# Eight chains a step for the latents' scan, and a new order of the work in its gaps

## The chip, the cores and the metric

The kernel runs on one core of a Trainium2 chip. The metric is the device time of one execution in microseconds. The engines are named as the profile names them: PE (TensorE, matrix products; PEld are its weight loads), DVE (VectorE), ACT (ScalarE), POOL (GpSimd) and SP (SyncE, which here only issues transfers). ACT and POOL issue transfers too; those of POOL go through a software queue, those of SP and ACT through hardware queues.

## The reference

One layer of a block with two branches over 1024 latent tokens that follow 256 context tokens, width 1024, all in float32. One input projection feeds both branches; branch A is RWKV-7 time mixing with 16 heads of 64, in both directions, branch B is retention. Sigmoid gates merge them, and an output projection follows.

```python
def step(S, inp):                       # branch A, one token
    w_t, k_t, v_t, kk_t, b_t = inp[:5]
    sa = jnp.einsum('bhvk,bhk->bhv', S, kk_t)
    S = (S * w_t[:, :, None, :] - sa[..., None] * b_t[:, :, None, :]
         + v_t[..., None] * k_t[:, :, None, :])
    o = jnp.einsum('bhvk,bhk->bhv', S, inp[5]) if with_out else None
    return S, o
...
o = head_norm((outs[0] + outs[1]).reshape(B, L, A_WIDTH), ln_w, ln_b, A_HEADS, A_GN_EPS)
...
merged = jax.nn.sigmoid(ma) * ya + jax.nn.sigmoid(mb) * yr
x = x + gate[:, None, :] * (merged @ w_out[l])
```

The latents' scans start from the final state of the context's scan in the same direction, so 32 scans (16 heads, two directions) of 1280 tokens are run.

## The kernel before

**Stages.** By the time of the span: projections and the preparation of branch A (0 to 820 us); the scans over the context, filled with the matmuls of retention's values, gv (820 to 1172); the scans over the latents, filled with the matmuls of the gates, gm (1172 to 1772); retention and the output of branch A (1772 to 2180); the output projections (to 2480). The change lies in the second and third stage, above all in the third.

**Scans in chunks.** A scan is cut into chunks of 64 tokens. Two heads share the 128 partitions; such a pair in one direction is a chain here, 8 pairs times 2 directions. A chunk's products between keys (A, in `chunk_mats`) are masked by DVE into ka (64 rows) and aa (128 rows); keys bk are then scaled by POOL and turned by PE against the identity (bt, in `chunk_turn`), with ACT moving them to SBUF. For each set of four chunks of eight pairs and directions the inverses of triangular matrices are needed: `inv_keys` makes the products B, `inv_vec` runs 31 pairs of operations (tmp, TL) and twelve 32x32 turns (E, TD, TN) on DVE, and `inv_join` makes the full inverses T from their quarters by two rounds of small products I. T is put together by ACT's copies.

**A step.** `chain_step` takes some chains one chunk further: X = keys times state sv, negated by ACT (xs); U = T times xs, copied by ACT (uv), with O, the queries' product with the state; S = the turned keys times uv, added by DVE to the decayed state sp (made by POOL) into the next sv, with O's second part. After each of the three products `gap()` flushes stores of finished gates and fills in as many gate matmuls as the remaining ones divided by the remaining gaps, so that PE has work while ACT and DVE make the next operand. Here a step has four chains (two pairs, two directions), 64 steps are run, and there are 192 gaps with some six gm each. The lambdas handed to `chain_step` put the next chunks' A, bt and the inverses' work into the gaps: `inv_gap(t)` counts 24 gaps for each inverse, calls `inv_keys` five times and `inv_join` twice in them and doles out `inv_vec` over about 24.

**What sets the order.** The kernel is written in a language where a scheduler orders instructions by dependencies and priorities, but `late` adds an order: an operation marked so comes on its engine behind the last PE instruction, or behind the last one that `lead` named for "v" (DVE) or "a" (ACT). So the lead operations (sv, xs, uv) stand ahead of what was written after them with `late(.., "v")`, such as the inverses' tmp and TL, whereas the masks were not leads. Pools limit the buffers: pA has four PSUM buffers (for A, bt, B, I), gates have three gp buffers on the way to memory.

**Outputs.** Outputs of four chains and two chunks leave PSUM together; `put` copies (first half of the groups) or adds (second half, when the two directions meet) into oT, a buffer of all 1024 tokens of two pairs, which is stored once per two pairs, by SP and at the end by POOL.

Of the kernel before, what the change touches and what calls it, by code (L numbers as in the profile page):

```python
# [49 lines left out]
MF = 3.0  # L50
# [78 lines left out]
class Kern:  # L129
# [588 lines left out]
    def v_proj(self, dst, hi, lo):  # L718

        nc = self.nc  # L720
        for t in range(0, 10, 2):
# [14 lines left out]
            nc.scalar.dma_start(dst[t * P:(t + 2) * P, :].rearrange("(i q) c -> q i c", q=P), st)  # L736
# [62 lines left out]
    def subs(self, n):  # L799

        if n < 2:
            return [(p, d, 0) for p in range(4 * n, 4 * n + 4) for d in range(2)]
        pp, half = divmod(n - 2, 2)
        return [(p, d, NCU + 8 * half + 4 * q) for q in range(2) for p in (2 * pp, 2 * pp + 1) for d in range(2)]
# [83 lines left out]
    def inv_vec(self, job):  # L888
# [22 lines left out]
        for i in range(0, 32, 8):  # L911
# [6 lines left out]
            self.late(nc.scalar.copy(t[b:b + 32, :, 0:32], tdq[b:b + 32]), "a")  # L918
            yield TV
# [5 lines left out]
    def inv_join(self, job):  # L925

        nc, ts, tn = self.nc, job["t2"], job["TN"]
        pis = [self.pA.tile([P, 16, 32], F32, tag="A", name=self.nm("I")) for _ in range(2)]
        at = lambda q, b: 64 - b if q else b
        for l in range(16):  # L930
            for q, t in enumerate(ts):
                for b in (0, 64):
                    o = at(q, b) + 32
                    self.mm(pis[q][o:o + 32, l, :], t[b:b + 32, l, 32:64], tn[b:b + 32, 16 * q + l, :], start=True, stop=True)
        for q, t in enumerate(ts):
            for b in (0, 64):
                o = at(q, b) + 32
                self.late(nc.scalar.mul(t[b + 32:b + 64, :, 0:32], pis[q][o:o + 32], -1.0), "a")
        yield
        pis = [self.pA.tile([P, 16, 32], F32, tag="A", name=self.nm("I")) for _ in range(2)]  # L940
        for l in range(16):
            for q, t in enumerate(ts):
                for b in (0, 64):
                    o = at(q, b)
                    self.mm(pis[q][o:o + 32, l, :], t[b + 32:b + 64, l, 0:32], t[b + 32:b + 64, l, 32:64], start=True, stop=True)
        for q, t in enumerate(ts):
            for b in (0, 64):
                o = at(q, b)
                self.late(nc.scalar.copy(t[b:b + 32, :, 32:64], pis[q][o:o + 32]), "a")
                nc.gpsimd.memset(t[b + 32:b + 64, :, 0:32], 0.0)  # L950
        yield

    def inv_gap(self, t):
# [26 lines left out]
        if g == 16:  # L980
# [3 lines left out]
    def chunk_loads(self, p, u0, d=None, extra=False):  # L984
# [4 lines left out]
        odd = p % 2 if d is None else d  # L989
        ka = (self.wp if extra else rw).tile([P, 3, 4, C], F32, tag=f"ka{odd}", name=self.nm("ka"), bufs=2 - extra)  # L990
# [6 lines left out]
        two = lambda t: t.rearrange("q (d u) c -> q d u c", d=2)  # L997
        nc.sync.dma_start(two(bk), self.bkD[p].rearrange("d q u c -> q d u c")[:, :, u0:u0 + 2, :])
        o = C * (u0 - NCU)
        kr = lambda rows, a: self.krD[p, :, rows, a, o:o + 2 * C].rearrange("d q j -> q d j")  # L1000
        pair = lambda t: t.rearrange("q (d u) c -> q d (u c)", d=2)
        for h, ch, va in self.HEADS:
            nc.sync.dma_start(pair(ka[ch, 2 * h]), kr(ch, 0))
        nc.sync.dma_start(pair(ka[:, 1]), kr(slice(0, P), 1))
        scale = self.pc[:, p, :, u0:u0 + 2].rearrange("q d (u o) -> q d u o", o=1)
        return bk, ka, scale, False

    def chunk_mats(self, loads):
# [5 lines left out]
        if ctx:  # L1014
# [6 lines left out]
            nc.gpsimd.tensor_tensor(bk, bk, scale.broadcast_to([P, 4, 2 * C]), op=ALU.mult)  # L1021
        else:
# [3 lines left out]
            for i in range(4):  # L1026
                for h, ch, va in self.HEADS:
                    self.mm(pas[h][:, i], bk[ch, i, :], ka[ch, h:h + 2, i, :], start=True, stop=True)
            for h, ch, va in self.HEADS:
# [3 lines left out]
                nc.vector.tensor_tensor(aa[:, h], pa[:, :, 1 - h], m, op=ALU.mult)  # L1033
            b4 = bk.rearrange("q (d u) c -> q d u c", d=2)
            nc.gpsimd.tensor_tensor(b4, b4, scale.broadcast_to([P, 2, 2, 2 * C]), op=ALU.mult)
# [3 lines left out]
    def chunk_turn(self, mats):  # L1039
# [6 lines left out]
        for h in range(2):  # L1046
            nc.scalar.mul(bt[:, :, C * h:C * h + C], pt[:, :, C * h:C * h + C], self.mask[:, 3 * C + h:3 * C + h + 1])

    def chain_step(self, chains, sv, uv, pcs, extra, new=None, out=None):
# [4 lines left out]
        nc, rw = self.nc, self.rw  # L1054
        px = self.pC.tile([P, 4, C], F32, tag="C", name=self.nm("X"))
# [3 lines left out]
        xs = rw.tile([P, 4, C], F32, tag="xs", name=self.nm("xs"), bufs=1)  # L1059
# [538 lines left out]
```

## Time and profile before

| | us |
|---|---|
| median of 3 runs (lowest, highest) | 2477.68 (2475.95, 2483.03) |
| the profiled execution, own time | 2481.7 |
| its span | 2479.9 |
| mean granted clock of TensorE | 0.989 |
| PE, PEld busy over the span | 2384.1, 1925.7 |
| DVE, ACT, POOL busy | 1597.4, 1162.4, 576.3 |

Busy times are shares of one span and overlap. A row of the profile gives the engine, the line, the operation, the result and the operands by their names in the program, and then busy time, mean duration, and the idle time before it with what ended it. A float32 matmul of one kind shows two records. A line L557 is the helper `mm`, so that groups are told apart by the names of the tiles.

### The profile page before, as it was taken

How to read it: one execution, taken by the hardware profiler on the slowest of the kernel's cores; microseconds unless marked ns; L12 is line 12 of the kernel's file. 1: busy time of each engine (PE TensorE's matmuls, PEld its weight loads, DVE VectorE, ACT ScalarE, POOL GpSimd, SP SyncE). 2: the span in 40 equal slices, each digit the busy share in tenths (PEclk: the TensorE clock that was granted, in tenths of full speed). 3: DMA queues.
4: the chain of work that ended last, by engine and by line, in shares of the span. 5: the costliest groups of instructions: out<-in, count | busy, mean ns of one | idle time of the engine just before them, and what ended most of it. 6: DMA issues, size and time to landing. Idle time of an engine off the chain costs nothing. (4 is left out here: it accounts for less than half of the span.)

```text
span 2479.9 us, 53486 instructions
## 1 busy us (share of the span) xinstructions
PE 2384.1 (96%) x21200; PEld 1925.7 (78%) x21200; DVE 1597.4 (64%) x2834; ACT 1162.4 (47%) x2547; POOL 576.3 (23%) x720
## 2 busy tenths in 40 slices
PE   7999999999999999998999999999898998999998
PEld 4888888888888899987777777777666765688786
DVE  5486787777676244353988878783278657754644
ACT  6444344434443434445665556644356435543422
POOL 2221111112122011221222222223276335400000
PEclk9999999999999999998999999999899999999999
DMA  6154454455346625344555565553465654585552
GB/s 252 50 158 116 140 165 124 135 157 140 124 136 182 194 79 147 106 133 129 171 164 169 155 189 168 155 159 117 124 194 169 214 169 151 180 287 170 186 171 85
DMA packets 337708, 385.07 MB, mean 155 GB/s; under 512 B 87466, under 2 KB 240818, under 8 KB 334386
## 3 DMA queue, kind: packets, MB, share of 16 engines
q1 hardware_dynamic: 304370, 298.80, 39.2%
q0 software_dynamic: 12992, 55.58, 8.5%
q10 hardware_dynamic: 20096, 27.27, 3.1%
q8 instruction: 167, 2.74, 0.5%
q14 instruction: 83, 0.68, 0.1%
HBM read 264.63 MB, written 116.92 MB: 154 GB/s over the span
## 5 line engine op out<-in xcount | busy, mean ns | idle before, releaser
L330 PE MATMUL gm<-uh,wh 128*128 128x512 f32 x896 | 351.9, 394 | 5.3 <-ACT xp L402 3.3
L331 PE MATMUL gm<-ul,wh 128*128 128x512 f32 x896 | 352.1, 393 | 0.8 <-DVE ul L299 0.8
L332 PE MATMUL gm<-uh,wl 128*128 128x512 f32 x896 | 351.6, 392 | 0.0
L1065 POOL TENSOR_TENSOR sp<-sv,pc 64x256 f32<-64x256 f32 x152 | 105.0, 691 | 418.1 <-DVE sv L1089 197.9
L330 PEld LDWEIGHTS gm<-uh,wh 128*128 128x128 f32 x896 | 168.5, 188 | 39.7 <-ACT xp L402 3.7
L331 PEld LDWEIGHTS gm<-ul,wh 128*128 128x128 f32 x896 | 168.8, 188 | 38.1 <-issue 1.7
L332 PEld LDWEIGHTS gm<-uh,wl 128*128 128x128 f32 x896 | 168.6, 188 | 34.5
L660 DVE TENSOR_TENSOR wlo<-wraw,whi 128x256 fp32r<-128x256 f32 x168 | 79.4, 487 | 144.5 <-ACT whi L659 141.6
L557 PE MATMUL gm<-uh,wlo 128*128 128x512 f32 x416 | 171.2, 411 | 0.7 <-DVE wlo L660 0.7
L557 PE MATMUL gm<-uh,whi 128*128 128x512 f32 x416 | 171.4, 412 | 0.0
L557 PE MATMUL gm<-ul,whi 128*128 128x512 f32 x416 | 170.8, 411 | 0.0
L557 PE MATMUL gv<-wlo,uh 128*128 128x256 f32 x512 | 147.8, 289 | 1.5 <-issue 1.5
L557 PE MATMUL gv<-whi,ul 128*128 128x256 f32 x512 | 148.0, 289 | 0.0
L211 DVE TENSOR_TENSOR lo<-raw,hi 128x512 fp32r<-128x512 f32 x128 | 93.0, 731 | 85.4 <-ACT hi L210 85.2
L557 PE MATMUL gv<-whi,uh 128*128 128x256 f32 x512 | 147.8, 289 | 0.0
L210 ACT CAST hi<-raw 128x512 fp32r<-128x512 f32 x128 | 78.9, 622 | 140.4 <-PE yr L1277 76.2
L902 DVE TENSOR_TENSOR tmp<-E,TL 128x31 f32<-128x31 f32 (+15 forms) x310 | 131.0, 423 | 8.9
L904 DVE TENSOR_TENSOR TL<-TL,tmp 128x31 f32<-128x31 f32 (+15 forms) x310 | 128.2, 414 | 8.2
L1477 PE MATMUL ro<-s,rs 128*128 128x512 f32 x256 | 123.8, 596 | 4.8 <-DVE s L1431 4.4
L1079 ACT COPY uv<-U 64x256 f32<-64x256 f32 x160 | 58.8, 367 | 146.5 <-PE U L557 87.3
L1089 DVE TENSOR_TENSOR sv<-S,sp 64x256 f32<-64x256 f32 x144 | 60.7, 422 | 98.3 <-PE S L557 65.4
L210 ACT CAST wh<-wr 128x1024 fp32r<-128x1024 f32 x56 | 58.8, 1051 | 132.6 <-PE gm L331 104.6
(297 smaller groups left out, 6206.9 us busy)
## 6 DMA issues: line engine op xcount, KB each, us to landing
wr<-in_w_in SPq DMA_DIRECT2D x56, 512.0 KB
wraw<-in_w_in SPq DMA_DIRECT2D x84, 256.0 KB
bk<-bkD SPq DMA_DIRECT2D x80, 256.0 KB
krD<-kr POOLq DMA_DIRECT2D x16, 1024.0 KB, 4.6
raw<-in_wr SPq DMA_DIRECT2D x64, 256.0 KB
vtD<-vt POOLq DMA_DIRECT2D x64, 160.0 KB, 4.2
bkD<-bk POOLq DMA_DIRECT2D x32, 320.0 KB, 6.7
bkD<-bk POOLq DMA_DIRECT2D x16, 640.0 KB, 6.5
```

What stands on the lines that cost most here:

```text
L210: nc.scalar.copy(hi, src)
L211: (eng or nc.vector).tensor_tensor(lo, src, hi.bitcast(F32), op=ALU.subtract)
L330: nc.tensor.matmul(acc[:, :n], hi[:, k, :], self.hi(k, t0, n), start=(k == 0), stop=False)
L331: nc.tensor.matmul(acc[:, :n], hi[:, k, :], self.lo(k, t0, n), start=False, stop=False)
L332: nc.tensor.matmul(acc[:, :n], lo[:, k, :], self.hi(k, t0, n), start=False, stop=(k == KT - 1))
L557: return self.pin(self.nc.tensor.matmul(*a, **k))
L660: self.late(nc.vector.tensor_tensor(lo[:, j % size, k:k + 2], r, h.bitcast(F32), op=ALU.subtract), "v")
L902: self.late(nc.vector.tensor_tensor(t3, et[:, j + 1:, j:j + 1].broadcast_to([P, n, m]), tl[:, j:j + 1, 0:m].broadcast_to([P, n, m]), op=AL ...
L904: self.late(nc.vector.tensor_tensor(tl[:, j + 1:, 0:m], tl[:, j + 1:, 0:m], t3, op=ALU.subtract), "v")
L1065: nc.gpsimd.tensor_tensor(sp[ch], sv[ch, h], pcs[ch].broadcast_to([64, 4, C]), op=ALU.mult)
L1089: self.lead("v", nc.vector.tensor_tensor(new[h], ps[ch], sp[ch], op=ALU.add))
L1477: nc.tensor.matmul(po, qx[d][:, k, cols], st[:, k, :], start=(d == 1 and k == 0), stop=False)
```

## The change

1. A step has eight chains, four pairs with two directions, and one chunk: 32 steps, 96 gaps with twice the matmuls. `subs`, `lat_loads`, `lat_values`, `chunk_loads`, `chain_step` and `rwkv_lat` follow; loads take pieces of one chunk where they took two.
2. A is computed in two halves of 64 columns; the masks for aa become leads of DVE, the copies of bt leads of ACT. In a step's first gap stand A of the next chunks' first half and all turns of the next step's keys (`turns`), in the second the other half's A (`products`), in the third the outputs (`outputs`).
3. `inv_gap` counts 12 gaps for an inverse and doles out `inv_vec` over ten of them. `inv_join` makes its first round in gap 11 and its second in the next step's `turns`, each cut in the middle by `fill(0.6)`, three gm. Half of T's copies go from ACT to POOL.
4. Stores of gates and of values are issued by POOL in place of ACT.
5. oT becomes og, of two chunks and four pairs, stored every second step by POOL and, for the second half, loaded back by SP ahead of the addition.
6. MF, the filling between the pieces at the head of the latents, goes from 3.0 to 5.0.

On PE, a step in the midst of the latents before. X, A, U, O, B and S are the products named above, gm a gate matmul; the last number is how many like rows follow each other:

```order
L557 MATMUL X_14789<-sv_14316,ka_14141 64x64 x4
L557 MATMUL X_14789<-sv_14316,ka_14296 64x64 x4
L557 MATMUL A_14804<-ka_14614,bk_14613 128x128
L557 MATMUL A_14805<-ka_14614,bk_14613 128x128
...
L557 MATMUL gm_14786<-uh_97,wlo_14158 128x512
...
L557 MATMUL U_14839<-xs_14798,T_1314_11686 64x64 x2
L557 MATMUL O_14627<-ka_14141,sv_14316 64x64 x2
...
L557 MATMUL S_14912<-uv_14317,bt_14352 64x64 x4
```

and after:

```order
L557 MATMUL X_13977<-sv_13658,ka_13513 64x64 x8
L557 MATMUL X_13977<-sv_13658,ka_13519 64x64 x8
L557 MATMUL A_14000<-ka_13819,bk_13818 64x128
L557 MATMUL A_14001<-ka_13819,bk_13818 64x128
...
L1038 MATMUL bt_14024<-ident,bk_13512 128x128 x4
L1038 MATMUL bt_14031<-ident,bk_13518 128x128 x4
L557 MATMUL gm_13896<-ul_110,whi_13441 128x512
...
L557 MATMUL U_14062<-xs_13994,T_1246_11301 64x64 x2
L557 MATMUL O_13976<-ka_13513,sv_13658 64x64 x2
...
L557 MATMUL A_14098<-ka_13825,bk_13824 64x128
```

Blocks of X, U and O have twice the matmuls, an A has sixteen rows of 64 columns in place of eight of 128, both turns follow the first A, and the second A follows U and O; between A or the turns and the next block stand twelve gm where there were six or seven.

On DVE, between two updates of the state (sv) before, in a gap with the inverses' work:

```order
L1089 TENSOR_TENSOR sv_11924<-S_12394,sp_12293 64x4x64 x2
...
L660 TENSOR_TENSOR wlo_12430<-wraw_12433,whi_12429 128x256
L902 TENSOR_TENSOR tmp_12714<-E_12552,TL_12553 128x31
L904 TENSOR_TENSOR TL_12553<-TL_12553,tmp_12714 128x31
...
L702 SCALAR_TENSOR_TENSOR gp_12614<-gp_12614,gm_12427 128x512
L1032 TENSOR_TENSOR ka_12474<-A_12596,mask 64x256
L1033 TENSOR_TENSOR aa_12595<-A_12596,mask 128x256
```

and after, from one sv to the next masks:

```order
L1083 TENSOR_TENSOR sv_14316<-S_14652,sp_14347 64x512 x2
L902 TENSOR_TENSOR tmp_14689<-E_14479,TL_14480 128x192
...
L1224 TENSOR_TENSOR og_14323<-O_14322,og_14323 128x4x64 x2
...
L904 TENSOR_TENSOR TL_14480<-TL_14480,tmp_14698 128x21x11
L1026 TENSOR_TENSOR ka_14568<-A_14746,mask 64x256
L1027 TENSOR_TENSOR aa_14745<-A_14746,mask 128x256
...
L902 TENSOR_TENSOR tmp_14784<-E_14479,TL_14480 128x240
```

The inverses' operations of a gap stand behind the masks of that gap, and there are more of them in it.

On POOL, after (before, its queue in this stage held sp, bk and the memsets and, at its end, the last stores of oT):

```order
L1060 TENSOR_TENSOR sp_13685<-sv_13348,pc 64x512 x2
L1232 DMA oD<-og_12955 64x4x128 x4
L711 DMA grD<-gp_13650 128x512
L1028 TENSOR_TENSOR bk_13512<-bk_13512,pc 128x512
...
L918 COPY T_1313_11730<-TD_13882 32x16x32 x2
L918 COPY T_1314_11731<-TD_13882 32x16x32 x2
```

The stores of gates and outputs and half of T's copies now stand in one queue with sp and bk.

The diff, cut to its core:

```diff
-MF = 3.0
+MF = 5.0
...
-                self.begin(gates, 3 * 16 * NPAIR // 2, 0.0)
+                self.begin(gates, 3 * 16 * NPAIR // 4, 0.0)
...
-            self.late(self.nc.scalar.dma_start(dst, st), "a")
+            self.nc.gpsimd.dma_start(dst, st)
...
-            nc.scalar.dma_start(dst[t * P:(t + 2) * P, :].rearrange("(i q) c -> q i c", q=P), st)
+            nc.gpsimd.dma_start(dst[t * P:(t + 2) * P, :].rearrange("(i q) c -> q i c", q=P), st)
...
-            self.late(nc.scalar.copy(t[b:b + 32, :, 0:32], tdq[b:b + 32]), "a")
-            yield TV
+            nc.gpsimd.tensor_copy(t[b:b + 32, :, 0:32], tdq[b:b + 32])
+            yield 2 * TV
...
+        for first in (True, False):
+            pis = [self.pA.tile([P, 16, 32], F32, tag="A", name=self.nm("I")) for _ in range(2)]
+            for l in range(16):
+                if l == 8:
+                    self.fill(0.6)
+                for q, t in enumerate(ts):
+                    for b in (0, 64):
+                        o = at(q, b) + 32 * first
+                        lhs, rhs = (t[b:b + 32, l, 32:64], tn[b:b + 32, 16 * q + l, :]) if first else \
+                            (t[b + 32:b + 64, l, 0:32], t[b + 32:b + 64, l, 32:64])
+                        self.mm(pis[q][o:o + 32, l, :], lhs, rhs, start=True, stop=True)
             for q, t in enumerate(ts):
                 for b in (0, 64):
+                    o = at(q, b) + 32 * first
+                    if first:
+                        self.late(nc.scalar.mul(t[b + 32:b + 64, :, 0:32], pis[q][o:o + 32], -1.0), "a")
+                    else:
+                        self.late(nc.scalar.copy(t[b:b + 32, :, 32:64], pis[q][o:o + 32]), "a")
+                        nc.gpsimd.memset(t[b + 32:b + 64, :, 0:32], 0.0)
+            yield
...
-        per, g = divmod(t, 24)
+        per, g = divmod(t, 12)
         last = 1 + NPAIR
         n = 4 + per
-        if g == 1 and n <= last:
+        if g == 0 and n <= last:
             self.jobs[n] = {}
             self.keys = self.inv_keys(n, self.jobs[n], self.wp)
-        if g in (1, 4, 7, 10, 13) and n <= last:
+        if g in (0, 1, 4, 7, 10) and n <= last:
             next(self.keys)
-        if g in (19, 22) and 3 + per <= last:
-            if g == 19:
-                self.join = self.inv_join(self.jobs[3 + per])
+        if g == 11 and 3 + per <= last:
+            self.join = self.inv_join(self.jobs[3 + per])
             next(self.join)
-        if t == 0 or g == 17:
-            n = 3 + per + (g == 17)
+        if g == 0:
+            n = 3 + per
             self.vec = self.inv_vec(self.jobs[n]) if n <= last else iter(())
-            self.vec_us, self.vec_gaps, self.owed = 12 * TV + sum(map(self.sub_us, range(31))), 24 if t else 17, 0.0
+            self.vec_us, self.vec_gaps, self.owed = 16 * TV + sum(map(self.sub_us, range(31))), 10, 0.0
         self.owed += self.vec_us / self.vec_gaps
         while self.owed > 0.0:
             us = next(self.vec, None)
             if us is None:
                 break
             self.owed -= us
-        if g == 16:
+        if g == 9:
...
-        two = lambda t: t.rearrange("q (d u) c -> q d u c", d=2)
-        nc.sync.dma_start(two(bk), self.bkD[p].rearrange("d q u c -> q d u c")[:, :, u0:u0 + 2, :])
+        nc.sync.dma_start(bk, self.bkD[p:p + 2, :, :, u0, :].rearrange("a d q c -> q (a d) c"))
         o = C * (u0 - NCU)
-        kr = lambda rows, a: self.krD[p, :, rows, a, o:o + 2 * C].rearrange("d q j -> q d j")
-        pair = lambda t: t.rearrange("q (d u) c -> q d (u c)", d=2)
+        kr = lambda rows, a: self.krD[p:p + 2, :, rows, a, o:o + C].rearrange("a d q j -> q (a d) j")
         for h, ch, va in self.HEADS:
-            nc.sync.dma_start(pair(ka[ch, 2 * h]), kr(ch, 0))
-        nc.sync.dma_start(pair(ka[:, 1]), kr(slice(0, P), 1))
-        scale = self.pc[:, p, :, u0:u0 + 2].rearrange("q d (u o) -> q d u o", o=1)
+            nc.sync.dma_start(ka[ch, 2 * h], kr(ch, 0))
+        nc.sync.dma_start(ka[:, 1], kr(slice(0, P), 1))
+        scale = self.pc[:, p:p + 2, :, u0:u0 + 1].rearrange("q a d o -> q (a d) o")
...
-                for h, ch, va in self.HEADS:
-                    self.mm(pas[h][:, i], bk[ch, i, :], ka[ch, h:h + 2, i, :], start=True, stop=True)
+                for c in (slice(0, C), slice(C, 2 * C)):
+                    for h, ch, va in self.HEADS:
+                        self.mm(pas[h][c, i], bk[ch, i, c], ka[ch, h:h + 2, i, :], start=True, stop=True)
...
-                nc.vector.tensor_tensor(aa[:, h], pa[:, :, 1 - h], m, op=ALU.mult)
-            b4 = bk.rearrange("q (d u) c -> q d u c", d=2)
-            nc.gpsimd.tensor_tensor(b4, b4, scale.broadcast_to([P, 2, 2, 2 * C]), op=ALU.mult)
+                self.lead("v", nc.vector.tensor_tensor(aa[:, h], pa[:, :, 1 - h], m, op=ALU.mult))
...
-            nc.scalar.mul(bt[:, :, C * h:C * h + C], pt[:, :, C * h:C * h + C], self.mask[:, 3 * C + h:3 * C + h + 1])
+            self.lead("a", nc.scalar.mul(bt[:, :, C * h:C * h + C], pt[:, :, C * h:C * h + C], self.mask[:, 3 * C + h:3 * C + h + 1]))
...
+            def turns():
+                if s != 8:
+                    self.send(outs)
+                if n and n % 4 == 0:
+                    next(self.join, None)
+                if n < last:
                     nxt.append(self.chunk_mats(ld.pop(0)))
+                for m in mats:
+                    self.chunk_turn(m)
+                self.inv_gap(3 * n)
+
+            def products():
+                if n < last:
+                    nxt.append(self.chunk_mats(ld.pop(0)))
+                    if n + 1 < last:
+                        ld.extend(self.lat_loads(n + 2, a) for a in range(2))
+                self.inv_gap(3 * n + 1)
+
+            def outputs():
+                self.put(po, og, s)
+                if s % 2:
+                    outs.append((r, s, og))
+                if s == 7:
+                    self.send(outs)
+                self.inv_gap(3 * n + 2)
+            if s % 2 == 0:
+                og = self.wp.tile([P, 2, 4, 2, C], F32, tag="og", name=self.nm("og"), bufs=2)
+                if s >= 8:
+                    self.move(r, s + 1, og, nc.sync, True)
+            self.chain_step(chains, sv, uv, pcs, (turns, products, outputs), dst, po)
...
+    def put(self, po, og, s):
+        src = po.rearrange("p (a d) c -> p a d c", d=2)
+        for dst, x in ((og[:, 0, :, s % 2], src[:, :, 0]), (og[:, 1, :, 1 - s % 2], src[:, :, 1][:, :, ::-1])):
+            if s < 8:
+                self.nc.scalar.copy(dst, x)
             else:
+                self.nc.vector.tensor_tensor(dst, x, dst, op=ALU.add)
+    def move(self, r, s, og, eng, load):
+        for d, t0 in ((0, C * (s - 1)), (1, LAT - C * (s + 1))):
+            for h, ch, va in self.HEADS:
+                mem = self.oD[4 * r:4 * r + 4, ch, t0:t0 + 2 * C].rearrange("p q t -> q p t")
+                sb = og[va, d].rearrange("q p u c -> q p (u c)")
+                eng.dma_start(*((sb, mem) if load else (mem, sb)))
+    def send(self, outs):
+        for r, s, og in outs:
+            self.move(r, s, og, self.nc.gpsimd, False)
+        outs.clear()
```

More of the change, by code (lines that the diff above doesn't have):

```diff
@@ L802, in subs @@
             return [(p, d, 0) for p in range(4 * n, 4 * n + 4) for d in range(2)]
-        pp, half = divmod(n - 2, 2)
-        return [(p, d, NCU + 8 * half + 4 * q) for q in range(2) for p in (2 * pp, 2 * pp + 1) for d in range(2)]
+        r, q = divmod(n - 2, 4)
+        return [(p, d, NCU + 4 * q) for p in range(4 * r, 4 * r + 4) for d in range(2)]
     def inverse(self, n):
@@ L931, in inv_join @@
             for q, t in enumerate(ts):
                 for b in (0, 64):
[L933 to L950, printed above, removed]
@@ L1072, in chain_step @@
             if out is not None:
-                po, first, last = out
                 for h, ch, va in self.HEADS:
-                    self.mm(po(va, ci), sv[ch, h, ci, :], rho[ch], start=(first and ci == 0), stop=False, skip_group_check=True)
+                    self.mm(out[va, ci], sv[ch, h, ci, :], rho[ch], start=(ci == 0), stop=False, skip_group_check=True)
         with self.tc.high_priority(offset=URGENT):
@@ L1092, in chain_step @@
                 for h, ch, va in self.HEADS:
-                    self.mm(po(va, ci), uv[:, h, ci, :], aa[:, h, :], start=False, stop=(last and ci == 3), skip_group_check=True)
+                    self.mm(out[va, ci], uv[:, h, ci, :], aa[:, h, :], start=False, stop=(ci == m - 1), skip_group_check=True)
         extra[2]()
@@ L1134, in chain_ctx @@
             else:
-                end = rw.tile([P, 4, C], F32, tag="xs", name=self.nm("send"), bufs=1)
+                end = rw.tile([P, 8, C], F32, tag="xs", name=self.nm("send"), bufs=1)[:, :4]
                 dst = [end[ch] for h, ch, va in self.HEADS]
@@ L1226, in put @@
-    def put(self, po, oT, g):
-        nc = self.nc
-        f = oT[:, :, P * g:P * g + P]
-        r = oT[:, :, LAT - P * g - P:LAT - P * g][:, :, ::-1]
-        for d, o in enumerate((f, r)):
-            src = po.rearrange("p (a d) u c -> p a d (u c)", d=2)[:, :, d]
-            if g < 4:
-                nc.scalar.copy(o, src)
-            else:
-                nc.vector.tensor_tensor(o, src, o, op=ALU.add)
+        last, og, outs = 2 * 16 - 1, None, []
+        for n in range(last + 1):
+            r, s = divmod(n, 16)
+            t2 = self.t2[2 + 4 * r + s // 4]
+            chains = [(ka[:, :, i], ka[:, 1, i], aa[:, :, i], bt[:, i], t2[a][:, 4 * i + s % 4, :])
+                      for a, (ka, aa, bt, bk) in enumerate(mats) for i in range(4)]
+            sv, uv = vals
+            if n < last:
+                vals = self.lat_values(n + 1)
+            dst = [vals[0][ch, h] for h, ch, va in self.HEADS] if s < 15 else None
+            pcs = self.pc[:, 4 * r:4 * r + 4, :, NCU + s:NCU + s + 1].rearrange("q p d o -> q (p d) o")
+            po = self.pO.tile([P, 8, C], F32, tag="O", name=self.nm("O"))
+            nxt = []
+            def turns():
[4 more added lines that the diff above has]
+                if n < last:
+                    nxt.append(self.chunk_mats(ld.pop(0)))
+                for m in mats:
+                    self.chunk_turn(m)
+                self.inv_gap(3 * n)
+            def products():
+                if n < last:
+                    nxt.append(self.chunk_mats(ld.pop(0)))
[14 more added lines that the diff above has]
+            self.chain_step(chains, sv, uv, pcs, (turns, products, outputs), dst, po)
+            mats = nxt
```

97 lines of the change are left out of this document (27 added, 70 removed).

## The prediction

> **What bounds the kernel now.** I read the page first (span, engine totals), then busy time by stage, then the waits of TensorE in the stage that the change rewrites, and last the timeline of one of its steps.
>
> ```profile
> span 2479.9 us, 53486 instructions
> ```
>
> ```profile
> 1172.00:1772.00 600.00, 588.53 (x10050) 459.50 (x10051) 447.99 (x1045) 337.06 (x895) 163.72 (x209) 1.00 0.54 156
> ```
>
> The columns after the length are the busy times of PE, PEld, DVE, ACT and POOL, then the granted clock, the DMA share and GB/s. The second row is the stage of the latents' chains: PE is busy for 588.5 of 600 us at clock 1.00, DVE for 448, ACT for 337, POOL for 164. So here only PE's own time counts, and what would make PE wait. The waits of PE in these 600 us are small:
>
> ```profile
> PE B L557 <- DMA bi<-bkD: 5.1, 5, 2.0
> PE S L557 <- issue: 3.5, 4, 1.0
> PE X L557 <- DVE sv L1089: 1.4, 2, 1.1
> ```
>
> Hence the gain must come from PE's order itself. One step of four chains, by the start of each group:
>
> ```profile
> 1401.53 0.69 PE L557 MATMUL X<-sv,ka 128*64 128x64 f32 x16
> 1402.15 1.16 PE L557 MATMUL A<-ka,bk 64*128 64x128 f32 x16
> 1403.24 0.50 PE L557 MATMUL gm<-uh,wlo 128*128 128x512 f32 x1
> 1403.58 0.40 PE L557 MATMUL gm<-uh,whi 128*128 128x512 f32 x1
> 1403.81 0.39 PE L557 MATMUL gm<-ul,whi 128*128 128x512 f32 x1
> ...
> 1404.73 0.39 PE L557 MATMUL gm<-uh,wlo 128*128 128x512 f32 x1
> 1405.05 0.27 PE L557 MATMUL U<-xs,T 64*64 64x64 f32 x2
> 1405.06 0.27 PE L557 MATMUL O<-ka,sv 64*64 64x64 f32 x2
> 1405.15 0.23 PE L557 MATMUL U<-xs,T 64*64 64x64 f32 x2
> ...
> 1405.52 0.23 PE L557 MATMUL O<-ka,sv 64*64 64x64 f32 x2
> 1405.67 0.50 PE L557 MATMUL gm<-uh,whi 128*128 128x512 f32 x1
> ...
> 1406.94 0.40 PE L557 MATMUL gm<-uh,wlo 128*128 128x512 f32 x1
> 1407.27 0.69 PE L557 MATMUL S<-uv,bt 128*64 128x64 f32 x16
> 1407.78 0.64 PE L557 MATMUL O<-aa,uv 128*64 128x64 f32 x16
> 1408.35 0.66 PE L1045 MATMUL bt<-ident,bk 128*128 128x128 f32 x4
> ...
> 1410.32 0.39 PE L557 MATMUL X<-sv,ka 128*64 128x64 f32 x6
> ```
>
> Busy times overlap, so I use distances between starts. Within a stretch of gate matmuls (gm) they are 0.23 apart (1403.58 to 1403.81). The first one takes 0.34 (1403.24 to 1403.58), and from the last one to the next small product pass 0.32 (to U) or 0.33 (to S). A stretch thus costs 0.11 + 0.09 = 0.20 us beside its matmuls. The step is 8.79 us (1401.53 to 1410.32), and there are 64.
>
> **Fewer, longer gaps: what PE saves.** Eight chains a step leave the number of X, U, O, S, A and gm matmuls as it is; they stand in half as many blocks. Gaps go from 192 to 96; each of the 14 halves of the seven joins is cut by three gm, which adds 14 stretches. 192 - 110 = 82 fewer, times 0.20: -16.4 us. The blocks have an opening of their own. X takes 0.62 for 16 records (1401.53 to 1402.15) and S, behind the same kind of gap, 0.51; I take 0.12 of X as opening, 32 X blocks fewer: -4. U with O: eight quadruples, 0.10 for the first and about 0.06 for each later one ((1405.52 - 1405.15) / 6), closed by 0.15 to the gm. Two such blocks become one, which saves 0.04 + 0.15 a pair; in 31 steps the second A, in tiles of the same 64x64 kind, stands right behind it, and I take another 0.07 there: -0.26 x 32 = -8.3. S with O: 0.51 + 0.57, of which I take 0.15 as the turn from one kind of block to another, 31 fewer: -4.7. The gm inside the joins cause 14 more switches: +2. Sum -31.4.
>
> **The A product in halves.** 16 records of 64x128 tiles take 1.09 us (1402.15 to 1403.24), two tiles side by side; after, 32 records in 64x64 tiles. That U and O of both heads start 0.01 apart and a whole quadruple takes 0.06 says that four 64x64 tiles run together; then the same columns stream for the same time. Bounds: 0, and 1.09 more for each of 62 products (one pair of tiles at a time). I take 0, since the U/O rows are the same form.
>
> **Inverses in 10 of 12 gaps, masks and transposed keys first.** Ahead, the work of one inverse on DVE was spread over about 24 gaps; now ten gaps of twice the length carry it, that is 3.33 of every 4 steps.
>
> ```profile
> L902 DVE TENSOR_TENSOR tmp<-E,TL 128x31 f32<-128x31 f32 (+15 forms) x217 | 97.3, 449 | 6.1
> L904 DVE TENSOR_TENSOR TL<-TL,tmp 128x31 f32<-128x31 f32 (+15 forms) x217 | 94.2, 434 | 5.6
> L1032 DVE TENSOR_TENSOR ka<-A,mask 64x256 f32<-64x256 f32 x124 | 51.7, 417 | 17.2 <-PE A L557 15.6
> ...
> L896 DVE STREAM_TRANSPOSE E<-D 128x256 f32<-128x256 f32 x28 | 15.5, 607 | 13.6 <-ACT D L883 12.9 <-ACT T L918 0.5
> ```
>
> An inverse has 31 pairs of L902 and L904 (0.883 us, 27.4) and twelve turns like L896 (0.607, 7.3): 34.7 us, 10.4 a loaded step. All else on DVE is 448 - 7 x 34.7 = 205 us, 6.4 for each of 32 steps. So DVE needs 16.8 us in a step of about (600 - 31) / 32 = 17.8: 94%. It does not bind on the mean, but the masks (two products, four operations each, 0.42 apiece), the states sv and the outputs' additions come in clumps; masks ahead of the inverses' work now end before the next gap's work starts, and sv, queued on DVE behind tmp and TL, is what comes late: the next step's X waits for it, and with X the whole of PE. Bounds 0 and +30 (the second rival); I take 0.35 in each of 23 loaded steps, +8.
>
> **Joins and PSUM.** Seven times the second half of a join, two products and two turns share the four pA buffers within two gaps; the turns wait for ACT to empty the join's two.
>
> ```profile
> L918 ACT COPY T<-TD 32x512 f32<-32x512 f32 x28 | 17.3, 618 | 0.3
> ...
> L949 ACT COPY T<-I 32x512 f32<-32x512 f32 x28 | 16.2, 578 | 2.5 <-PE I L557 2.1
> ```
>
> Four L949 copies are 2.3 us; the product between hides about 1.1 of that and the masks' own wait part of the rest. Bounds 0 and 7 x 2.3 = 16; I take 0.7 each, +5. Half of the T copies (28, 0.62 us each on ACT) go to GpSimd: ACT loses 17 us that no one waits for.
>
> **Stores and outputs.** ACT loses 51 gate stores and SP most of 16 stores of outputs; POOL gets the former, 64 shorter stores of outputs, and the copies. POOL is busy for 164 of 600 us, so it has room, and three gp buffers give the stores a delay of some 11 us (24 gm of 0.23 a buffer, two buffers ahead). SP gets 32 loads of the outputs' first half, each asked for long before the addition; the store that the first of them needs was sent a step earlier. The keys, values and outputs now travel in pieces of half the size; the DMA share of 0.54 leaves room. Late landings I put at +3 (bounds 0 and 10). Of the old waits shown above, 10 us, I let all go: the keys are loaded elsewhere and a longer gap covers the states; if they stay, that is the upper end.
>
> **The start of retention.** SP's five loads of rs take 36 us there, and the waits of SP's queue name the gate stores; TensorE waits at the end of that chain.
>
> ```profile
> 1743.44 36.08 SPq L1388 DMA_DIRECT2D rs<-kD  x5
> ```
>
> ```profile
> SPq L1388 <- DMA maD<-gp: 18.4, 2, 9.8
> ```
>
> ```profile
> PE st L1416 <- ACT kx L1401: 12.3, 4, 8.8
> ```
>
> With the gate stores on GpSimd's queue the loads need not wait for ACT's. Bounds 0 and -8.8; I take -5. MF at 5.0 and the vst stores move fills and issues within the two heads, where the same number of gm is run later or earlier: 0, between -4 and +4.
>
> **Sum.** -31.4 for PE's order, +8 +5 +3 -10 for waits, -5 for retention: -30.4. The profiled execution took 2481.7 us (span 2479.9), 4.0 above the median of 2477.68 of the three runs. 2481.7 - 30.4 = 2451.3 profiled, 2447 against the median.
>
> **Rivals.** (1) *No new waits.* The masks are the only thing that TensorE needed early and they now come first; then +8 +5 fall away: 2434. For it speaks the 6% that DVE has left, against it the clumps.
> (2) *DVE becomes the bound.* In these rows GpSimd and DVE hold each other up:
>
> ```profile
> 1402.96 0.41 DVE L902 TENSOR_TENSOR tmp<-E,TL 128x240 f32<-128x240 f32 x1
> 1403.40 0.41 DVE L904 TENSOR_TENSOR TL<-TL,tmp 128x240 f32<-128x240 f32 x1
> 1403.85 1.14 DVE L902 TENSOR_TENSOR tmp<-E,TL 128x247 f32<-128x247 f32 x1
> ```
>
> ```profile
> 1403.48 1.24 POOL L1035 TENSOR_TENSOR bk<-bk,pc 128x512 f32<-128x512 f32 x1 [1.67 <-issue]
> ```
>
> The tmp that starts inside a scaling of bk takes 0.73 longer. A step has four such GpSimd operations (two bk, two sp). If every one stops an inverse's operation for 0.73, that is 2.9 a step; 0.6 of it is in the means already ((0.449 - 0.41 + 0.434 - 0.41) x 31 / 3.33). DVE then needs 16.8 + 2.3 = 19.1 of 17.8 us, +1.3 in 23 loaded steps: +30 in place of the +8 that I took, 2469, at the edge of what can be told from no change. It decides once the collisions cost over 1 us a step. Against it: the T copies come when DVE turns TN, and the masks read PSUM.
> [...]
> (3) *Slower: A's halves do not run four abreast.* With one pair of tiles at a time a product takes 2.18 in place of 1.09 us: +68 for 62, 2515. It decides from 30.4 / 62 = 0.49 us more a product. The U/O rows speak against it; they have 64 columns a record and A has 128.
> (4) *The change does nothing for retention:* the rs loads wait for something else; 2452, inside the range.
>
> **Chances.** Forecast with (4) 0.52, rival 1 0.23, rival 2 0.13, rival 3 0.07, others (a late store or load that blocks a buffer over and over) 0.05. A change of 0.3%, 7.4 us, is about what a measurement tells here: faster is below 2470.2, slower above 2485.1. Faster 0.81: the forecast, rival 1 and half of rival 2; same 0.09, the other half and some of the others; slower 0.10, rival 3 and the rest of the others. The range goes from just below rival 1, 2431, to a little beyond rival 2, 2474.
>
> **What would show it.** Right: some 36 gm a step in three long stretches; A 32 records in 1.1 us; X 32 records in about 1.1; the stage some 25 to 32 us shorter; PE's waits in it 15 to 20 us, led by sv and by the A or bt that waits for T copies; the 8.8 us wait of st shrunk. Wrong: A records with starts 2.2 us apart in all; waits on sv or masks beyond 30 us; DVE without idle time in loaded steps; or waits on GpSimd's stores.

## The result and the profile after

The changed kernel takes 2467.66 us, the median of 5 runs (2460.66 to 2468.66); the kernel before took 2483.01 us in the 5 runs beside them (2475.95 to 2483.11). The ratio is 0.9929 with a 95% interval from 0.9911 to 0.9946: faster by 0.7%, about 17 us (the two medians are 15.4 us apart). The forecast was 2447 us and a gain of 30.7: the sign and the range held, the size was nearly twice too large. Part of the distance in microseconds is the base: the three runs shown ahead of the change had a median of 2477.68, later medians of the same kernel were 2481.5 to 2483.9. So the profiled execution of before, 2481.7 us, did not stand above the median, and the 4.0 us that the forecast took off for it were wrong. The rest is in the trace.

Span, engine totals and clock of the changed kernel, as on the page of before:

```profile
span 2465.6 us, 55584 instructions
PE 2356.7 (96%) x22224; PEld 1927.3 (78%) x22224; DVE 1570.7 (64%) x2774; ACT 1120.5 (45%) x2411; POOL 682.8 (28%) x852
PEclk9999999999999899989999999999999999999999
```

PE is busy 27 us less than before. More instructions stand on it, the halves of A. Busy time by stage, the first row of before, the others of after (length; PE, PEld, DVE, ACT, POOL; granted clock, DMA share, GB/s):

```profile
820.00:1172.00 352.00, 335.16 (x4374) 313.24 (x4375) 141.62 (x360) 158.01 (x430) 48.89 (x68) 0.98 0.45 129
```

```profile
820.00:1172.00 352.00, 336.27 (x4355) 314.63 (x4355) 140.03 (x359) 143.41 (x395) 87.16 (x121) 0.95 0.44 126
1172.00:1772.00 600.00, 567.37 (x11121) 467.76 (x11119) 430.55 (x994) 317.98 (x806) 236.42 (x293) 0.99 0.69 178
```

Fixed stretches mix the stages once they are shorter, so I also took the starts of three landmarks from the two traces:

| | before | after | difference |
|---|---|---|---|
| first gv to first gm of the gates (context) | 330.9 | 340.9 | +10.0 |
| first to last gm of the gates (latents) | 625.1 | 604.5 | -20.7 |
| last gm of the gates to the end | 708.4 | 704.8 | -3.6 |

The sum is -14.3 us, the difference of the spans. The latents gain, but less than the forecast's 25; the context stage loses in this execution what the forecast held unchanged.

The waits of PE in the latents after (1150 to 1750 us of the span; totals, how often, the longest):

```profile
PE X L557 <- issue: 13.2, 11, 2.6
PE I L557 <- issue: 5.5, 8, 2.0
PE bt L1038 <- POOL T L947: 3.0, 6, 0.6
PE X L557 <- DVE sv L1083: 2.1, 2, 1.6
PE gm L557 <- issue: 1.6, 1, 1.6
PE A L557 <- issue: 1.1, 1, 1.1
```

With the smaller rows they are 29.0 us; before, the same stretch of time had 15.1 us, nearly all of it at B and S:

```profile
PE B L557 <- DMA bi<-bkD: 9.1, 9, 2.9
PE S L557 <- issue: 3.5, 4, 1.0
```

The stage is 20.7 us shorter in spite of 13.9 us more waiting, so the order of PE itself brought about 34.6. X alone waits 15.3 us. Most of that is put down to "issue", that is to nothing the profile names; here is a wait for which it names sv, and a longer one for which it does not, then the rows of DVE and POOL beside the latter:

```profile
1313.27 1.15 PE L557 MATMUL X<-sv,ka 128*64 128x64 f32 x32 [1.60 <-DVE sv L1083]
1314.36 1.10 PE L557 MATMUL A<-ka,bk 64*64 64x128 f32 x32
1315.39 1.09 PE L1038 MATMUL bt<-ident,bk 128*128 128x128 f32 x8
...
1363.10 1.15 PE L557 MATMUL S<-uv,bt 128*64 128x64 f32 x32
...
1370.71 1.15 PE L557 MATMUL X<-sv,ka 128*64 128x64 f32 x32 [2.58 <-issue]
```

```profile
1362.11 1.43 DVE L902 TENSOR_TENSOR tmp<-E,TL 128x255 f32<-128x255 f32 x1
1362.19 1.06 POOL L1028 TENSOR_TENSOR bk<-bk,pc 128x512 f32<-128x512 f32 x1
1363.58 0.42 DVE L904 TENSOR_TENSOR TL<-TL,tmp 128x255 f32<-128x255 f32 x1
1364.04 0.43 DVE L1026 TENSOR_TENSOR ka<-A,mask 64x256 f32<-64x256 f32 x1
...
1365.48 0.41 DVE L902 TENSOR_TENSOR tmp<-E,TL 128x256 f32<-128x256 f32 x1
...
1368.88 0.42 DVE L904 TENSOR_TENSOR TL<-TL,tmp 128x247 f32<-128x247 f32 x1
1369.21 1.40 DVE L1083 TENSOR_TENSOR sv<-S,sp 64x512 f32<-64x512 f32 x2
```

sv ends at 1370.61 and X starts at 1370.71, so the unnamed wait is sv as well. DVE never pauses here. S is done at 1364.25, but DVE is still at the masks of the second A, held up by a tmp that took 1.43 us beside GpSimd's scaling of bk, and then runs the tmp and TL of the second gap before it comes to sv, 5 us late.

Four steps of the changed kernel, each from the start of its first X to the start of the next (columns as above), show where DVE is full:

```profile
1257.20:1277.15 19.95, 18.84 (x433) 15.69 (x432) 13.84 (x35) 11.80 (x31) 6.58 (x9) 1.00 0.52 139
1277.15:1295.23 18.08, 16.44 (x301) 13.69 (x301) 17.34 (x38) 9.42 (x26) 3.96 (x5) 1.00 0.68 174
1295.23:1313.27 18.04, 16.44 (x300) 13.72 (x301) 17.27 (x42) 8.71 (x25) 8.29 (x11) 1.00 0.62 165
1313.27:1332.10 18.83, 18.66 (x430) 15.43 (x431) 9.44 (x20) 13.75 (x33) 11.87 (x15) 1.00 0.90 216
```

In the second and third DVE is busy for 17.3 us of 18.1 and PE for 16.4; in the fourth, which has none of the inverses' tmp and TL, DVE has half of its time free.

### The profile page after: what moved, and what is told of

It is laid out like the page before. It is cut to its first block, busy times and chain, and to the rows that moved or that the text cites. A ratio compares the mean times of both kernels' runs of the same rounds, so it can differ in the third digit from the quotient of the medians.

```text
span 2465.6 us, 55584 instructions
## 1 busy us (share of the span) xinstructions
PE 2356.7 (96%) x22224; PEld 1927.3 (78%) x22224; DVE 1570.7 (64%) x2774; ACT 1120.5 (45%) x2411; POOL 682.8 (28%) x852
## 3 DMA queue, kind: packets, MB, share of 16 engines
q0 software_dynamic: 23104, 87.05, 12.4%
## 4 chain that ended last, share of the span: by engine, by line
PE 82%; DVE 5%; DMA 5%; issue 3%; ACT 2%; POOL 1%; SPq 1%; DVEq 0%; ACTq 0%; POOLq 0%
PE gm L557 10%; PE gm L330 9%; PE gm L331 9%; PE gm L332 9%; PE gv L557 9%; PE ro L1479 4%; PE A L557 3%; PE yr L1279 2%; PE yr L1280 2%; PE yr L1278 2%; PE X L557 2%; PE bt L1038 2%; PE S L557 1%; PE O L557 1%; PE I L557 1%
## 5 line engine op out<-in xcount | busy, mean ns | idle before, releaser
L1060 POOL TENSOR_TENSOR sp<-sv,pc 64x512 f32<-64x512 f32 (+1 forms) x92 | 89.5, 973 | 175.4 <-DVE sv L1083 153.9
L902 DVE TENSOR_TENSOR tmp<-E,TL 128x31 f32<-128x31 f32 (+15 forms) x310 | 117.0, 377 | 8.4
L456 POOL DMA_DIRECT2D vtD<-vt x64 | 46.1, 767 | 240.5 <-ACT vt L452 240.5
L1433 DVE SCALAR_TENSOR_TENSOR s<-s,ph,st 128x512 f32<-128x512 f32 x128 | 91.1, 739 | 33.8 <-PE st L1420 29.0
```

Of the source, the lines that this page charges most:

```text
L902: self.late(nc.vector.tensor_tensor(t3, et[:, j + 1:, j:j + 1].broadcast_to([P, n, m]), tl[:, j:j + 1, 0:m].broadcast_to([P, n, m]), op=AL ...
L1060: nc.gpsimd.tensor_tensor(sp[ch], sv[ch, h], pcs[ch].broadcast_to([64, m, C]), op=ALU.mult)
L1433: nc.vector.scalar_tensor_tensor(new[:, k], old[:, k], self.cd[:, d, h:h + 1], a, op0=ALU.mult, op1=ALU.add)
```

## Experiments

All in this table are the changed kernel with one to three edits; the ratio is to the kernel before, run beside them. The changed kernel has 0.9929 and 15.3 us. Waits are those of 1150 to 1750 us.

| | median, us | ratio | interval | X waits, us |
|---|---|---|---|---|
| values' stores on ACT | 2465.09 | 0.9925 | 0.9913 to 0.9937 | 18.5 |
| weights 1.1, 0.55, 1.3 | 2457.82 | 0.9898 | 0.9882 to 0.9915 | 9.0 |
| whole A | 2466.74 | 0.9937 | 0.9919 to 0.9954 | 10.2 |
| gates' stores on ACT | 2463.40 | 0.9920 | 0.9903 to 0.9937 | 14.9 |
| half of the pairs | 2449.02 | 0.9866 | 0.9841 to 0.9892 | 2.9 |
| bk scaled by ACT | 2454.27 | 0.9886 | 0.9868 to 0.9904 | 5.7 |
| T's copies on ACT | 2461.43 | 0.9927 | 0.9899 to 0.9955 | 16.6 |
| no leads | 2467.79 | 0.9942 | 0.9930 to 0.9955 | 6.0 |
| bk by ACT and weights | 2451.06 | 0.9862 | 0.9836 to 0.9888 | 1.0 |
| the same, eleven gaps | 2443.15 | 0.9846 | 0.9818 to 0.9875 | 0 |
| no gm in the joins | 2468.54 | 0.9939 | 0.9915 to 0.9962 | 16.8 |

**Where X's wait comes from: fewer pairs.**

```diff
         for j in range(31):
             n, m = 31 - j, j + 1
+            if job.get('half') and j % 2:
+                continue
...
+            if n <= last:
+                self.jobs[n]['half'] = True
...
-            self.vec_us, self.vec_gaps, self.owed = 16 * TV + sum(map(self.sub_us, range(31))), 10, 0.0
+            self.vec_us, self.vec_gaps, self.owed = 16 * TV + sum(map(self.sub_us, range(0, 31, 2))), 10, 0.0
```

This kernel leaves out 15 of the 31 pairs tmp and TL of each inverse, so it shows only what their time on DVE costs.

> The changed kernel with every second of the 31 pairs tmp and TL left out of the latents' inverses (their result is then another). A loaded step loses some 4 us of DVE work of 17. Theory 3 (DVE's queue makes sv, and so X, late): the waits of X, 15.3 us in the latents' stage, fall below 4 us; with them goes half clock that follows them, so the time falls by 12 to 20 us against the changed kernel, to 2446 to 2454. The other theory, that X waits for something else (loads of ka, ACT, PSUM): the waits of X stay above 10 us, the time within 4 us.

The waits of X fell from 15.3 to 2.9 us and the time to 2449.02, the forecast of theory 3. The whole list of X:

```profile
PE X L557 <- DVE sv L1087: 2.9, 1, 2.9
```

It is DVE's backlog, and with it gone the changed kernel is 1.3% faster than before, near the forecast's 1.2%.

**The same work, dealt otherwise.**

```diff
-        self.owed += self.vec_us / self.vec_gaps
+        self.owed += self.vec_us / self.vec_gaps * (1.1, 0.55, 1.3)[g % 3]
```

> The changed kernel with one thing other: the inverses' work on DVE is dealt over the same ten gaps, but unevenly: 1.1 of the mean in a step's first gap, 0.55 in the second (ahead of sv), 1.3 in the third (behind sv). The amount of work is the same. Theory 3 (sv stands behind the second gap's tmp and TL on DVE): the waits of X, 16.4 us in the latents of the changed kernel, fall below 6 us and the time falls by 8 to 14 us. Theory 4 (DVE has too much to do in these steps, or GpSimd's operations stop it): the same waits come at other places, at A or at U, and the time changes by less than 4 us.

```profile
PE X L557 <- issue: 7.9, 9, 1.4
PE A L557 <- issue: 5.3, 4, 1.5
```

Neither theory alone. X's waits fell by 6 us, not below 6, and nearly 6 us of waiting turned up at A (7.6 us in three rows, where it was 1.8); yet the time fell by about 8 us, to 0.9898. In the two profiles the latents are only 2.9 us shorter (601.6 in place of 604.5), while the context, which the edit does not touch, is 8.4 us shorter. So the waits speak for theory 4, and where most of the 8 us comes from is not shown. The waits of X also became shorter, 1.4 us at most in place of 2.6, which the section on the hardware returns to.

**GpSimd beside DVE.**

```diff
-        nc.gpsimd.tensor_tensor(bk, bk, scale.broadcast_to([P, 4, 2 * C]), op=ALU.mult)
+        if ctx:
+            nc.gpsimd.tensor_tensor(bk, bk, scale.broadcast_to([P, 4, 2 * C]), op=ALU.mult)
+        else:
+            for i in range(4):
+                self.late(nc.scalar.mul(bk[:, i], bk[:, i], scale[:, i]), "a")
```

> The changed kernel with the scaling of bk in the latents done by ACT (four operations for each bk) in place of GpSimd. GpSimd's scalings no longer meet tmp on DVE. Theory 4 (GpSimd's reads stop DVE): in the changed kernel a tmp or TL next to a scaling takes some 1.0 us longer; 62 such collisions at most 60 us of DVE, so the mean of tmp falls from 0.38 us to about 0.34, the waits of X fall by more than half, and the time by 6 to 12 us, if ACT's 68 us more do not make xs and uv late. The other theory, that collisions fall in DVE's idle time: the waits of X change by less than 4 us, the time by less than 3, or rises with ACT.

tmp and TL in the changed kernel and in this one (1160 to 1740 us):

```profile
L904 DVE TENSOR_TENSOR TL<-TL,tmp 128x31 f32<-128x31 f32 (+15 forms) x217 | 92.0, 424 | 5.7
L902 DVE TENSOR_TENSOR tmp<-E,TL 128x31 f32<-128x31 f32 (+15 forms) x217 | 83.3, 384 | 5.6
```

```profile
L904 DVE TENSOR_TENSOR TL<-TL,tmp 128x31 f32<-128x31 f32 (+15 forms) x217 | 80.3, 370 | 5.6
L902 DVE TENSOR_TENSOR tmp<-E,TL 128x31 f32<-128x31 f32 (+15 forms) x217 | 78.1, 360 | 5.6
```

With the scaling gone from GpSimd, tmp and TL take 17 us less of DVE's time in the stage. The waits of X fell by 9.6 us, the time by some 11 us, to 2454.27, at the upper end of theory 4's range. ACT took the 62 scalings without making xs or uv late: S waits 0.3 us for uv, and none of PE's waits in the stage is for xs. In the trace of the changed kernel (1160 to 1740 us) the 19 tmp and 21 TL that ran beside a scaling took 0.66 and 0.93 us in the mean, the other 198 and 196 took 0.36 and 0.37; the masks ka and aa took 0.42 us with a scaling beside them (52 and 57) and without one (72 and 67).

**The same edit on the kernel before.**

> The kernel before, with bk's scaling in the latents by ACT in place of GpSimd. The collisions of tmp and scaling are there too (1.14 in place of 0.41 us), but DVE has 152 us idle in 600 spread over 24 gaps and X waits only 2 us for sv. If the collisions cost time only where DVE's queue is behind, as in the change's loaded steps: the mean of tmp and TL falls by some 0.06 us, the time by less than 3 us (or it rises by up to 4 with ACT's work). If collisions cost PE time by themselves: the time falls by 6 to 10 us as it did in the changed kernel.

```profile
L904 DVE TENSOR_TENSOR TL<-TL,tmp 128x31 f32<-128x31 f32 (+15 forms) x217 | 83.5, 385 | 5.6
L902 DVE TENSOR_TENSOR tmp<-E,TL 128x31 f32<-128x31 f32 (+15 forms) x217 | 79.1, 365 | 6.1
```

From 0.449 and 0.434 us: DVE is relieved of 29 us, more than in the changed kernel, and the time does not move: 2483.55 against 2483.62 us, ratio 1.0 (0.9984 to 1.0015). ACT's new work costs something here: S waits for uv 6.3 us where it waited 0.5, so the 0 is a net figure; but X, which is what waits for sv, had only 2.0 us to lose. The collisions are old; the change made them cost, because it took DVE's slack in the loaded steps.

**Both together, and eleven gaps.** The weights with the scaling on ACT, then also `vec_gaps` 11 with weights (1.15, 0.6, 1.3) and the rest of the work due at gap 10.

> The changed kernel with both edits that helped: bk's scaling by ACT, and the inverses' work dealt 1.1, 0.55, 1.3 over a step's gaps. Alone the first took the waits of X from 15.3 to 5.7 us, the second to 9.0 with 5.3 more at A. Theory 3 with 4 (one backlog on DVE behind all these waits): together the waits of X and A fall below 5 us and the time to 2447 to 2453 where the first alone has 2454. The other theory: the first has already taken all that DVE's backlog cost, the rest of the waits has other causes; 2452 to 2457.

> As the run before it, with the inverses' work over eleven gaps (weights 1.15, 0.6, 1.3), so that a loaded step has some 1 us less of it, but the turns TN end one gap ahead of the join's first half in place of two. If DVE's backlog still binds: 2 to 5 us below the run with ten gaps. If not: I waits for TN or for ACT's copies of T, 0 to 5 us above it.

X waits 1.0 us in the first and does not appear among the waits of the second, whose longest in the stage are these:

```profile
PE I L557 <- issue: 3.5, 3, 1.5
PE A L557 <- issue: 2.6, 3, 1.6
PE bt L1042 <- ACT T L946: 1.6, 3, 0.5
```

Together they take 2451.06, within theory 3's range of time; but A still waits 8.2 us in four rows, so the waits of X and A did not fall below 5, and the interval overlaps that of the scaling alone. With eleven gaps it is 2443.15 us. The intervals of these two overlap; both are clear of the changed kernel's, and the second, 1.5% faster than before (1.25 to 1.82%), is the best version found.

**The heaviest steps in five of these traces.** Of the latents' 32 steps, 14 carry 20 or more of the inverses' tmp and TL. Their means, worked out from the traces between the starts of one X and the next, in us:

| | step | DVE busy | PE waits |
|---|---|---|---|
| changed kernel | 17.5 | 16.75 | 1.15 |
| weights | 17.45 | 16.7 | 1.1 |
| bk by ACT | 16.6 | 15.7 | 0.4 |
| bk by ACT and weights | 16.4 | 15.5 | 0.2 |
| the same, eleven gaps | 16.35 | 15.4 | 0.1 |

Without its waits and what half clock takes, PE needs 16.2 to 16.3 us for such a step in all five. In the changed kernel DVE needs more than that, so these steps go at DVE's pace. Dealing the same work otherwise leaves that as it is, and the wait moves from X to A; taking the collisions out brings DVE below PE.

**The leads.** Without `lead` on the masks of aa and the copies of bt:

> The changed kernel with the masks of aa and the copies of bt no longer leads, so that the inverses' work of a gap may stand ahead of them on DVE and ACT as before the change. If the leads bring what the forecast took from them (masks and bt in time): A, bt and S wait for masks and copies, by 0.3 to 1 us a loaded step, and the time rises by 6 to 20 us. If PE needs neither early: the masks come later and sv earlier, the waits of X fall, and the time changes by -6 to +2 us.

```profile
PE A L557 <- issue: 11.3, 6, 2.3
PE X L557 <- issue: 3.3, 4, 1.2
PE X L557 <- DVE sv L1083: 2.7, 3, 1.3
```

The backlog moved from X to A (with 4.4 us in two further rows of A), and the time is 2467.79, 3 us worse by the ratio and not to be told from none. The leads choose who waits; they take nothing off DVE's list. My +6 to +20 was too much.

**A in whole tiles.**

```diff
-                for c in (slice(0, C), slice(C, 2 * C)):
-                    for h, ch, va in self.HEADS:
-                        self.mm(pas[h][c, i], bk[ch, i, c], ka[ch, h:h + 2, i, :], start=True, stop=True)
+                for h, ch, va in self.HEADS:
+                    self.mm(pas[h][:, i], bk[ch, i, :], ka[ch, h:h + 2, i, :], start=True, stop=True)
```

> The changed kernel with A in whole tiles of 64x128 again. By the prediction's row the 16 records take what the 32 halves take, some 1.1 us a product, and the second A of a step no longer stands in tiles of the same kind as U and O: the step from U/O to A goes from 0.04 us to some 0.15, and from A to B from 0.04 to 0.2, 31 and 24 times, so the time rises by 3 to 7 us. The other theory, that halves bring nothing: the time changes by less than 2 us.

0.9937 against 0.9929, intervals almost the same: the 3 to 7 us could not be told from none by the time.

**The stores and T's copies.** Three runs undo what went to GpSimd: the values' stores, the gates' stores, T's copies.

> The changed kernel with one thing undone: the stores of the values (vst) are issued by ACT again. In the order of the instructions this alone puts SP's loads of the context stage back: the fourth bk is again behind the second set of keys (kt, bi), not ahead of it. Theory 1 (order of SP's loads): in the changed kernel the keys for B land later, PE waits 9.4 us for them in the context stage (3.6 at 837.6) and TensorE's clock is granted at one half for 30.6 us there, against 7.2 and 10.2 us before; undone, the wait falls to some 7 us, the half clock to some 10 to 17 us, and the time by 5 to 12 us, to about 2458. Theory 2 (the half clock comes as it likes, whatever the order): the wait for B falls by 2 us, the half clock stays near 30 us, the time falls by 0 to 3 us.

> The changed kernel with the stores of the gates issued by ACT again. Theory 5 (these stores hold up SP's loads at the start of retention): the waits of st in its first 30 us, which fell from 12.3 us in all to less than 5, come back, and the time rises by 4 to 8 us. Theory 6 (retention's start has its own bound): those waits stay as they are in the changed kernel; ACT's 51 issues of 0.33 us stand ahead of some xs and uv, and the time changes by 0 to 3 us.

> The changed kernel with all of T's copies on ACT again. [...] If they cost DVE nothing: time within 3 us, waits of I and X the same. If they did: X waits fall by 3 us or more and the time by 3 to 8 us. A third case: ACT's copies now come in a row of four ahead of the join, so I waits for them and the time rises by 2 to 5 us.

None of the three moved the time beyond its interval (0.9925, 0.9920, 0.9927; the six times behind the last include one of 2483.64 us, without which it would be about 0.991). Theory 1 fell: with SP's order put back the wait of B in the context is 7.3 us in place of 9.4, and the time the same. Theory 5 fell as well. With ACT issuing the gates' stores SP's five loads of rs take 22.8 us, where they take 3.7 in the changed kernel (first row),

```profile
1734.61 3.66 SPq L1390 DMA_DIRECT2D rs<-kD  x5
1732.05 22.82 SPq L1390 DMA_DIRECT2D rs<-kD  x5
```

```profile
PE st L1418 <- ACT kx L1403: 8.1, 3, 4.9
```

and st waits 8.1 us between 1740 and 1830 us, where it waits 7.7 in the changed kernel and 12.3 before (not less than 5, as I had written). With T's copies on ACT, X waits 16.6 us in place of 15.3: on GpSimd they cost DVE nothing that shows there.

**The gm inside the joins.**

> The changed kernel without the three gm in the middle of each half of a join. By the forecast's price of a stretch 14 stretches in the latents go, -2.8 us, and the second half's products reach their copies earlier or later by 0.7 us only: the time changes by -4 to 0 us. If the three gm cover a wait (ACT's copies between the halves, PSUM): I and bt wait 0.7 us more at each of seven joins, +3 to +7 us.

```profile
PE I L557 <- issue: 10.7, 7, 2.7
```

I waits 5.2 us more; the time is 0.9939, not to be told from 0.9929. The three gm seem to cover waits of about what their stretches cost.

## Why the prediction was right and wrong

- **PE's order, -31.4: right.** The stage's -20.7 with +13.9 of waits leaves -34.6. That is a remainder, but it repeats: the stage less PE's waits and less half of its time at half clock is 606.0 and 603.4 us in the two kernels of the old order, 570.2 in the changed kernel and 568.7 to 572.9 in nine of its variants. The other two variants change PE's order themselves: whole A has 576.0, 5.8 more and within the 3 to 7 expected of it; without the gm in the joins it is 564.8. These are single profiles, but the two lie outside the spread of the rest.
- **A's halves, 0: right.** 1984 records in 62 products, and one takes 1.03 us by its starts (1314.36 to 1315.39) where it took 1.09; rival 3 is out.
- **DVE, +8: this is the step that failed.** X waits 15.3 us, A and the gm that needs wlo 2.8 more. The place was forecast rightly: sv comes late on DVE, behind tmp and TL, and X waits for it. What failed is the step from "It does not bind on the mean" to 0.35 us in each loaded step: 16.8 us of DVE in a step of 17.8 compares two means. In the 14 heaviest steps DVE needs 16.75 us, about as reckoned, but PE without its waits needs only 16.2, so DVE does bind there, and 16.1 of PE's 29 us of waits stand in these steps; PE's longer steps, 17.6 to 18.4 us in the mean, are the others. "DVE without idle time in loaded steps" was one of the signs of being wrong, and it showed. The runs bear it out: half of the pairs took 12.4 us from X's waits, the scaling on ACT 9.6.
- **Rival 2** had that condition right, DVE as the bound, but not its price: collisions did not become more (tmp and TL take 175.3 us, where they took 191.5), and DVE binds in 14 steps, not in 23. Its 2469 is close to the time measured by luck of the base: it is 9 us below the 2477.68 that it was worked out from, and the change gave 17. The gain lies between this and the forecast's 30.7.
- **Joins, +5:** I waits 5.5 us and bt 3.0, together 8.5. The place was right, the cause partly not: bt waited for the memsets on POOL.
- **Stores and loads, +3; old waits, -10:** no wait on a store shows in the latents; B's and S's waits of before are gone, 13 us there.
- **Retention, -5: right in size, not in reason.** From the last gm to the end it is 3.6 us less, and 1.8 to 8.9 less in the eleven runs on the changed kernel. SP's five loads take 3.7 us in place of 36, as forecast; but the run with the gates' stores on ACT shows that st no longer depends on it. What else made it earlier stays open.
- **Context, 0:** 340.9 us in the profiled execution but 329.0 to 337.0 in the eleven kernels with the edits above, against 330.9 before and 330.6 in the edit of before. So some 3 us are the change's, inside the -4 to +4; the other 7 belong to that execution.
- **The base, -4.0:** wrong, as told above.

In the sum: the waits of the latents came to +13.9 where +8 +5 +3 -10 were taken, 7.9 too little; the order of PE gave 3.2 more than forecast, the context cost some 3. So -30.4 becomes about -23, and the ratio says -17 with 4 to either side. The last 2 to 5 us I cannot assign: they are no more than two executions of one kernel differ by.

## What to carry to other kernels

Longer gaps save PE's switches (34.6 us here, with the rest of PE's new order), but they also lengthen the list that every other engine works off between two operations that PE needs. Ahead of such a change compare, for the busiest other engine, what it has to do in the heaviest step with what PE has to do in that same step; the means of a stage, 16.8 against 17.8 us here, hid steps of 16.75 against 16.2. Where the other engine is over, take work from it; to deal the same work to another gap moved the wait from X to A. The collisions of two engines cost nothing here as long as the one that they stopped had slack: the same edit was worth 0 us net in the kernel before and some 11 in the changed one.

## What the runs showed of the hardware

A short wait of PE could cost more than itself. The clock records of the trace have TensorE at one half in pieces of 3.4 us or two or three times that, and 20 of the 22 pieces in the profiles of the two kernels begin during a wait of PE of 0.9 us or more, or less than 1.8 us behind one:

```profile
841.17 1.14 PE L557 MATMUL B<-kt,bi 64*64 64x64 f32 x20 [3.36 <-DMA bi<-bkD]
```

```profile
840.00:860.00 20.00, 18.83 (x209) 18.26 (x210) 2.10 (x6) 10.08 (x35) 1.43 (x2) 0.84 0.44 125
```

The half clock sets in at 839.6, while PE waits 3.4 us for bi, and lasts 6.8 us, so that the clock is 0.84 over the 20 us from 840. In the latents a wait of 2.05 us was followed by 3.4 us at one half:

```profile
1412.33 0.39 PE L557 MATMUL I<-T 32*32 32x32 f32 x24 [2.05 <-issue]
1412.65 1.90 PE L557 MATMUL A<-ka,bk 64*64 64x128 f32 x32
1414.49 1.97 PE L1038 MATMUL bt<-ident,bk 128*128 128x128 f32 x8
```

A and bt, 1.10 and 1.09 us in the rows at 1314.36 and 1315.39, take 1.90 and 1.97. The context stage of the changed kernel's profile has 30.7 us at one half beside the 6.8 with which it begins in both, that of before 10.2; the difference at half speed is about the 10 us that it lost. The wait of 2.58 us ahead of the X at 1370.71 was likewise followed by 3.4 us at one half, the one of 1.85 us ahead of the X at 1665.26 by none. B's wait for its loads in the context is 4.1 us in one of these traces and 9.4 in another (gates' stores on ACT and the changed kernel), though the edit between them lies in the next stage, and three such waits of the changed kernel had 6.8 us each at one half with them, which adds to such chances. That this is why executions of equal code differ by some 7 us was not tested by itself. Between the even dealing and the weights, the pieces at one half from 815 to 1780 us fell from 54.6 to 30.7 us in the two profiles (granted clock over the span 0.986 and 0.991), and part of that edit's gain may be this. In the mean over all executions the clock does not explain the gap to the forecast: span times one minus the granted clock is 33.0 us in the changed kernel's five and 32.5 us in eleven of the kernel before.
